# Down projection of the MLP: groups 1 to 3 as seven block products for eight, with the residual rows kept in device memory meanwhile

## The chip, the core and the metric

The kernel runs on one core of a Trainium2 chip. A core has five engines that run their own instruction streams and meet through semaphores: PE (the 128 x 128 matmul array), DVE (element-wise work on two operands), ACT (element-wise work on one operand), POOL and SP (here both only start DMA transfers). The metric is the device time of one execution, in microseconds. Before the change it is 1384.47 us (median of three runs, 1383.11 to 1384.7).

## The reference

One transformer-like block on 512 tokens of width 1024, all in fp32. A gated delta rule with 8 heads and a retention with 4 heads are mixed, and an MLP follows. What matters here is its end:

```
mix = (sigmoid(gate_a) * ya + sigmoid(gate_b) * yb) @ w_out        # w_out 1024 x 1024
x   = x + rmsnorm(mix, n_mix_post)                                 # the residual rows, 512 x 1024
hn  = rmsnorm(x, n_mlp_pre)
ff  = square(relu(hn @ w_up)) @ w_down                             # w_up 1024 x 4096, w_down 4096 x 1024
return x + rmsnorm(ff, n_mlp_post)
```

## The kernel before

**Products.** An fp32 product is emulated by three matmuls (`mm3`, L80): each operand is split into a high part, rounded to the short type fp32r, and a low part, the rest; hi·hi, hi·lo and lo·hi are summed in PSUM. One matmul has a 128 x 128 weight operand and a moving operand of 512 or 256 columns.

**Weights.** All weights stream from device memory in blocks of 512 KB (128 x 1024 fp32, two K tiles of 512 columns). SP starts the load into a tile `raw` (L93, L144), ACT casts the high part `whi` (L110), DVE subtracts to get the low part `wlo` (L111). There are three `whi`/`wlo` pairs in a ring, so a split can be at most three blocks ahead of PE, and two to four `raw` buffers.

**Seven block products.** `seven` (L175) multiplies a 2 x 2 block matrix with seven block products in place of eight (the scheme of Winograd). It needs sums of the quarters of the activations (s1 to s4) and sums of the quarters of the weights (1 to 4). Its products come in a fixed order: 11, s2, 12, s1, s3, 22, s4, two weight blocks each. Quarter (0,0) of the result leaves after "12", (1,1) after "s3", (1,0) after "22" and (0,1) after "s4". Before the change it serves the value and gate projections of the four retention heads, and the up projection of MLP groups 1 to 3.

**Weight sums.** The sums of weight quarters are made in device memory, before they are needed: SP copies a quarter half (512 KB) into a buffer `sums` (L129), and POOL starts a DMA that adds another quarter onto it (L155, `add_blocks`). The copies are paced: `weights` issues one behind each of its loads as long as the list `trickle` is longer than `later_copies[0]`. `later_copies` is 24 at first and 0 from the end of the first retention head on.

**The MLP.** The 4096 hidden columns go in four groups of 1024 (`grp` 0 to 3). In each, the up projection makes squares of relu(hn @ w_up), split into high and low parts as soon as they leave PSUM (`square_relu`, L1101 on: DVE L1105 and L1109, ACT L1108), and the down projection adds squares @ w_down to `facc`. Up of group 0 is plain (`feature_major`), up of groups 1 to 3 runs through `seven`. Down of groups 0 to 2 is plain (`token_major`, L237): eight weight blocks, 24 matmuls of 128x512 for each. Down of group 3 is `row_tiles` (L1007): all weights are split into tiles that stay (`keep`), and each tile of 128 tokens is finished with its norm and its store while the next is multiplied. `row_tiles` also does the product with `w_out` ahead of the MLP; `mix_done` there makes the residual rows `x2` and their normed features `hn`. `x2` stays in the SBUF tile `acc` to the end.

**Order.** A scheduler orders each engine's instructions ahead of time by priorities in program order; `high_priority(n)` moves an instruction forward (weight splits by 200), `keep_in_program_order` pins matmuls, `issue_after` pins a DMA behind another instruction. Each engine then works strictly in that order.

## Time and profile before

| | before |
|---|---|
| median of 3 runs | 1384.47 us |
| profiled execution, its own time | 1384.53 us |
| span of that execution | 1382.8 us |
| PE busy | 1361.0 us, 7102 instructions |
| DVE busy | 923.4 us, 1599 instructions |
| ACT busy | 621.4 us, 1128 instructions |
| moved by DMA | 214.76 MB, mean 155 GB/s |

In the span, up of group 0 runs from about 1028 to 1077 us, down of group 0 to 1121, then up and down of group 1 to 1162 and 1205, of group 2 to 1246 and 1289, up of group 3 to 1329, its down to 1376, and the last norm and stores to the end. The product with `w_out` lies ahead of these, from about 984. Since `grp` counts from 0 and the words of the change from 1, "group 1" of the change is `grp` 0; from here on groups are called by `grp`.

A busy PE in the profile has matmuls in its pipeline, and the durations of single matmuls overlap; what a matmul costs is the pitch in a stage without waits, and not its own duration.

### The profile page before, as it was taken

The page shows a single profiled execution, that of the slowest core. Times are in us where ns is not written, and L with a number is a line of the kernel's source. Part 1 is how long each engine was busy: PE and PEld are TensorE (multiplying, and loading weights), DVE is VectorE, ACT ScalarE, POOL GpSimd, SP SyncE. Part 2 cuts the span into 40 slices and gives each one's busy share as a digit, 9 for nine tenths or more (in the row PEclk, how much of TensorE's full clock was granted, in tenths as well). Part 3 has the DMA queues.
Part 4 walks back from the last instruction along what each step waited for, and adds up shares of the span by engine and source line. Part 5 has one row for each costly group of instructions (what it writes and reads, how often), then busy time and mean ns, then how long its engine had stood idle before and what let it go on. Part 6 is the DMA issues. An engine that isn't in the chain of part 4 may idle for free.

```text
span 1382.8 us, 18650 instructions
## 1 busy us (share of the span) xinstructions
PE 1361.0 (98%) x7102; PEld 1135.8 (82%) x7102; DVE 923.4 (67%) x1599; ACT 621.4 (45%) x1128; POOL 110.5 (8%) x160
## 2 busy tenths in 40 slices
PE   8999999999999999999999999999999999999997
PEld 6888788778887888888888888888888899898986
DVE  5599889963675567567477576675788447374575
ACT  5777564624543323353453343443365444242441
POOL 1112200221011002000000000011011000000000
PEclk9999999999999999999999999999999999999999
DMA  5243625469458447784583873587739645353441
GB/s 160 71 143 116 194 83 170 118 141 240 109 122 161 115 144 167 176 271 155 146 283 90 200 244 104 162 226 156 242 95 226 159 137 153 102 182 113 143 133 61
DMA packets 101660, 214.76 MB, mean 155 GB/s; under 512 B 7135, under 2 KB 20593, under 8 KB 101058
## 3 DMA queue, kind: packets, MB, share of 16 engines
q1 hardware_dynamic: 85616, 170.41, 39.1%
q0 software_dynamic: 15232, 41.90, 16.5%
q8 instruction: 56, 0.92, 0.3%
q10 hardware_dynamic: 722, 1.25, 0.2%
q14 instruction: 34, 0.28, 0.1%
HBM read 207.77 MB, written 64.49 MB: 197 GB/s over the span
## 4 chain that ended last, share of the span: by engine, by line
PE 81%; DVE 9%; DMA 5%; ACT 3%; issue 1%; SPq 0%; DVEq 0%; ACTq 0%
PE mm L83 17%; PE mm L85 17%; PE mm L84 17%; PE mm L827 6%; PE dl L827 5%; PE mm L1127 4%; PE dl L1127 3%; DMA raw<-in_w_in_dram 3%; PE tr L289 2%; DVE wlo L111 2%; DVE c_y L477 1%; ACT whi L110 1%; PE dl L85 1%; PE dl L83 1%; PE dl L84 1%
## 5 line engine op out<-in xcount | busy, mean ns | idle before, releaser
L111 DVE TENSOR_TENSOR wlo<-raw,whi 128x1024 fp32r<-128x1024 f32 x250 | 305.5, 1223 | 293.9 <-ACT whi L110 291.9
L110 ACT CAST whi<-raw 128x1024 fp32r<-128x1024 f32 x250 | 262.8, 1052 | 465.8 <-PE mm L84 190.4
L84 PE MATMUL mm<-actT,whi 128*128 128x512 f32 (+1 forms) x528 | 207.9, 394 | 1.0 <-DVE actT L323 1.0
L85 PE MATMUL mm<-actT,wlo 128*128 128x512 f32 (+1 forms) x528 | 208.8, 396 | 0.0
L83 PE MATMUL mm<-actT,whi 128*128 128x512 f32 (+1 forms) x528 | 207.8, 395 | 0.6 <-ACT actT L322 0.6
L83 PE MATMUL mm<-whi,actT 128*128 128x512 f32 x344 | 136.2, 396 | 0.4 <-DVE r L1105 0.4
L84 PE MATMUL mm<-wlo,actT 128*128 128x512 f32 x344 | 135.8, 395 | 0.0
L85 PE MATMUL mm<-whi,actT 128*128 128x512 f32 x344 | 135.0, 394 | 0.0
L83 PEld LDWEIGHTS mm<-actT,whi 128*128 128x128 f32 x528 | 100.4, 190 | 20.6 <-ACT actT L322 1.1
L84 PEld LDWEIGHTS mm<-actT,whi 128*128 128x128 f32 x528 | 100.4, 190 | 20.2 <-DVE actT L323 1.3
L85 PEld LDWEIGHTS mm<-actT,wlo 128*128 128x128 f32 x528 | 100.6, 191 | 19.0
L83 PE MATMUL mm<-og,whi 128*128 128x512 f32 x256 | 99.8, 390 | 0.1
L84 PE MATMUL mm<-og,whi 128*128 128x512 f32 x256 | 99.7, 389 | 0.0
L85 PE MATMUL mm<-og,wlo 128*128 128x512 f32 x256 | 99.6, 389 | 0.0
L827 PE MATMUL mm<-whi,xsum 128*128 128x512 f32 x256 | 80.8, 389 | 0.0
L83 PEld LDWEIGHTS mm<-whi,actT 128*128 128x128 f32 x344 | 64.6, 188 | 14.6 <-DVE r L1105 0.8
L85 PEld LDWEIGHTS mm<-whi,actT 128*128 128x128 f32 x344 | 64.6, 188 | 13.2
L84 PEld LDWEIGHTS mm<-wlo,actT 128*128 128x128 f32 x344 | 64.6, 188 | 12.8
L477 DVE SCALAR_TENSOR_TENSOR c_y<-c_raw,convw,c_y 128x512 f32<-128x512 f32 x96 | 70.5, 750 | 3.4 <-ACT c_y L475 2.8
L1127 PE MATMUL mm<-hsum,whi 128*128 128x256 f32 x384 | 69.6, 283 | 0.0
L827 PE MATMUL dl<-whi,actT 128*128 128x512 f32 x192 | 61.1, 389 | 0.0
L1127 PEld LDWEIGHTS mm<-hsum,whi 128*128 128x128 f32 x384 | 59.9, 192 | 0.1
(323 smaller groups left out, 2506.1 us busy)
## 6 DMA issues: line engine op xcount, KB each, us to landing
raw<-in_w_in_dram SPq DMA_DIRECT2D x105, 512.0 KB, 4.1
raw<-sums SPq DMA_DIRECT2D x56, 512.0 KB, 3.7
sums<-in_w_in_dram SPq DMA_DIRECT2D x32, 512.0 KB, 5.3
raw<-in_w_down_dram SPq DMA_DIRECT2D x32, 512.0 KB, 4.5
raw<-in_w_up_dram SPq DMA_DIRECT2D x30, 512.0 KB, 3.8
sums<-sums POOLq DMA_DIRECT2D x28, 512.0 KB, 7.4
sums<-in_w_up_dram SPq DMA_DIRECT2D x24, 512.0 KB, 6.8
raw<-in_w_br_a_dram SPq DMA_DIRECT2D x16, 512.0 KB, 4.2
```

The costliest lines, as they stand in the source:

```text
L83: nc.tensor.matmul(ps, lh, rh, start=first, stop=False)
L84: nc.tensor.matmul(ps, lh, rl, start=False, stop=False)
L85: nc.tensor.matmul(ps, ll, rh, start=False, stop=last)
L110: nc.scalar.copy(hi[:, :n], raw[:, :n])
L111: nc.vector.tensor_tensor(lo[:, :n], raw[:, :n], hi[:, :n], ALU.subtract)
L289: nc.tensor.transpose(ps, src, ident)
L477: nc.vector.scalar_tensor_tensor(y, raw[:, j : j + T], tap(j), y, ALU.mult, ALU.add)
L827: m = nc.tensor.matmul(pss[t], lhs[i // 2], rhs[i % 2], start=first and k + i == 0, stop=k + i == 5, skip_group_check=not first,)
L1127: m = nc.tensor.matmul(pss[f // 2][:, ts], lhs[i // 2], rhs[i % 2], start=first and k + i + f % 2 == 0, stop=k + i == 5, skip_group_check= ...
```

## The change

The down projection of groups 0 to 2 runs through `seven` as well: 14 weight blocks of 12 matmuls each (168 matmuls) in place of 8 blocks of 24 (192). What comes with it:

- **Squares.** `Squares` keeps the squares of a group as fp32 in `r4` (four quarters: 11, 12, 21, 22, by token half and hidden half) next to the split quarters 11, 12 and 22, and makes the sums of quarters from them: `first_sums` (L1202 on, of the new kernel: s1, s2, s3, when 21 has left PSUM) and `last_sum` (L1210: s4, when 12 has). Each sum is split too (`split`: ACT cast, DVE L1122). For group 0 all of it is done in two steps of two feature tiles in the end of the plain up projection.
- **Sums of `w_down`.** 24 more copies (SP) and 24 more accumulating DMAs (POOL). `later_copies` is 48, 24 and then, from `w_out` on, 0. So the list that was empty after the attention stages is now worked off behind the eight loads of `w_out`, the twelve loads of up of group 0, and the first ones of its down. The accumulates of `dn0`, `up1`, `dn1`, `up2`, `dn2`, `up3` alternate by group, 18 behind the load of the residual, 8 after up of group 0 and 8 after up of group 1; the load of the last norm's weights comes behind the first 18.
- **Results.** `down_out` adds a quarter of the result to `facc` in one or two steps of 128x512 on DVE (on ACT or DVE for group 0).
- **Residual rows.** `mix_done` also writes each tile of `x2` to `x2_d` in device memory (ACT's queue, 512 KB each). The tile's room (`acc`) then holds sums of hn for the up projections, and before the last down projection POOL's queue loads the four tiles of `x2` back into it.
- **Tiles that stay.** The split weights of `w_out` and of the last down projection go to other tiles (`og`, `s4`, `r4`; `actT`, `s4`, `hn`, `r4`).
- **Sums of hn.** s1 takes the place of quarter 21 of hn itself, so it is written after the last plain up product has read that.

In all, matmuls of 128x512 go from 4602 to 4530, weight splits from 250 to 268, DVE instructions in the program from 1601 to 1689, ACT's from 996 to 1034; SP starts 42 more DMAs and POOL 28 more.

```diff
-    later_copies = [24]
+    later_copies = [48]
...
         if paced and i >= 13 and len(trickle) > later_copies[0]:
-            sums, part, k = trickle.pop(0)
-            with tc.issue_after(load.ins):
-                sums.copy(part, k)
+            copy_block(load)
...
+    def copy_block(load):
+        sums, part, k = trickle.pop(0)
+        with tc.issue_after(load.ins):
+            sums.copy(part, k)
...
     def block_weights(block):
...
-        nc.sync.dma_start(raw.rearrange("p (k c) -> p k c", k=2), block)
+        load = nc.sync.dma_start(raw.rearrange("p (k c) -> p k c", k=2), block)
+        if trickle and not later_copies[0]:
+            copy_block(load)
...
+    def token_product(quarters):
...
+        def product(pss, x, ks, wts, first):
+            wh, wl = wts
+            xh, xl = quarters[x]
+            for t in range(2):
+                tt = slice(t * P, (t + 1) * P)
+                for kk in range(2):
+                    k = 2 * ks + kk
+                    lhs, rhs = (xh[:, k, tt], xl[:, k, tt]), (wh[:, kk, :], wl[:, kk, :])
+                    for i in range(3):
+                        m = nc.tensor.matmul(
...
         def mix_done(t, ps):
             xn = add_normed(t, ps, wpost)
             y = norm_halves([(x2[:, t, hs], lambda half: None) for hs in hss])
+            nc.scalar.dma_start(x2_d[:, t, :], x2[:, t, :])
...
-        keeps = [None] * 3 + og_keeps() + ff_keeps() + facc_keeps()[:1]
+        keeps = [None] * 3 + og_keeps() + s4_keep() + four_keeps(pm, "r4")
+        later_copies[0] = 0
...
+            def first_sums(self, f):
+                fs = slice(f, f + 2)
+                r11, r21, r22 = self.r[:, 0, 0, fs, :], self.r[:, 0, 1, fs, :], self.r[:, 1, 1, fs, :]
+                nc.vector.tensor_tensor(r22, r21, r22, ALU.subtract)
+                nc.vector.tensor_tensor(r21, r11, r21, ALU.subtract)
+                nc.vector.tensor_tensor(r11, r22, r11, ALU.subtract)
+                for r, name in ((r11, "s2"), (r22, "s1"), (r21, "s3")):
+                    split(r, self.fs(name, f))
+
+            def last_sum(self, f):
+                r12 = self.r[:, 1, 0, f : f + 2, :]
+                nc.vector.tensor_tensor(r12, r12, self.r[:, 0, 0, f : f + 2, :], ALU.add)
+                split(r12, self.fs("s4", f))
+
+        def up_out(sq):
+            def out(th, ch, pss, u=(None, None), op=None):
+                for t in range(2):
+                    sq.quarter(ch, th, 2 * t, pss[t], u[t], op)
+                if not sq.last:
+                    for f in (0, 2):
+                        if (th, ch) == (1, 0):
+                            sq.first_sums(f)
+                        elif (th, ch) == (0, 1):
+                            sq.last_sum(f)
...
             if grp < 3:
-                for half in range(2):
-                    pss = token_major(w_down, ff_tile, half * 512, 8, grp * 8)
...
+                src = w_down[grp * D : (grp + 1) * D, :]
+                seven(src, 0, 512, down_sums[grp], token_product(sq.dst), temp, down_out(grp))
             else:
-                wk = og_keeps() + ff_keeps()
+                x2 = cp.tile([P, 4, D], F32, tag="acc", name="x2")
+                for t in range(4):
+                    nc.gpsimd.dma_start(x2[:, t, :], x2_d[:, t, :])
+                wk = four_keeps(act, "actT") + s4_keep()
```

**Order, DVE, where down of group 2 begins.** Weight splits are `wlo`; `r` is a square on its way to `actT`; `dl` and `mm` are PSUM banks; `p1` and `u2` partial sums of `seven`. The first row is the last weight split ahead of the squares that leave after the up product "22". Before:

```order
L111 TENSOR_TENSOR wlo_10025<-raw_10022,whi_10024 128x1024
L1142 TENSOR_TENSOR r_9938<-dl_9876,p1_9540 128x512
L1142 TENSOR_TENSOR r_9943<-dl_9877,p1_9541 128x512
L1105 SCALAR_TENSOR_TENSOR r_9938<-r_9938 128x512
L111 TENSOR_TENSOR wlo_10055<-raw_10052,whi_10054 128x1024
L1109 TENSOR_TENSOR actT_9539<-r_9938,actT_9538 128x2x256
L1105 SCALAR_TENSOR_TENSOR r_9943<-r_9943 128x512
L1142 TENSOR_TENSOR r_10008<-mm_9742,u2_9542 128x512
L111 TENSOR_TENSOR wlo_10085<-raw_10082,whi_10084 128x1024
L1109 TENSOR_TENSOR actT_9539<-r_9943,actT_9538 128x2x256
L1105 SCALAR_TENSOR_TENSOR r_10008<-r_10008 128x512
```

After, at the same place, the middle of the piece: `r4` are the kept squares, `ffq_9625` is s1, `ffq_9627` holds s2 and s3, and the last row begins the squares that leave after the up product "s4" (before: the row with `mm_9742`).

```order
L114 TENSOR_TENSOR wlo_10176<-raw_10173,whi_10175 128x1024
L1204 TENSOR_TENSOR r4_9623<-r4_9623 128x512
L1122 TENSOR_TENSOR ffq_9625<-r4_9623,ffq_9625 128x512
L1205 TENSOR_TENSOR r4_9623<-r4_9623 128x512
L114 TENSOR_TENSOR wlo_10194<-raw_10191,whi_10193 128x1024
L1122 TENSOR_TENSOR ffq_9627<-r4_9623,ffq_9627 128x512 x2
L1204 TENSOR_TENSOR r4_9623<-r4_9623 128x512
L114 TENSOR_TENSOR wlo_10214<-raw_10211,whi_10213 128x1024
L1205 TENSOR_TENSOR r4_9623<-r4_9623 128x512
L1122 TENSOR_TENSOR ffq_9625<-r4_9623,ffq_9625 128x512
L1122 TENSOR_TENSOR ffq_9627<-r4_9623,ffq_9627 128x512 x2
L114 TENSOR_TENSOR wlo_10232<-raw_10229,whi_10231 128x1024
```

Between the squares of "22" and those of "s4" there now stand the sums of the squares, their splits, and more weight splits. In full, from the split of `wlo_10136` (the place of `wlo_10025` before) to the first L1118 on the squares of "s4", DVE has seven weight splits and 21 operations of 128x512.

**Order, DVE, where down of group 0 begins.** Before:

```order
L111 TENSOR_TENSOR wlo_9349<-raw_9346,whi_9348 128x1024
L1109 TENSOR_TENSOR actT_8828<-r_9262,actT_8827 128x512
L1109 TENSOR_TENSOR actT_8828<-r_9267,actT_8827 128x512
L1105 SCALAR_TENSOR_TENSOR r_9272<-mm_9140,r_9272 128x512
L1105 SCALAR_TENSOR_TENSOR r_9277<-mm_9141,r_9277 128x512
L1109 TENSOR_TENSOR actT_8828<-r_9272,actT_8827 128x512
L1109 TENSOR_TENSOR actT_8828<-r_9277,actT_8827 128x512
L111 TENSOR_TENSOR wlo_9379<-raw_9376,whi_9378 128x1024
```

After, the same squares of the second half of the hidden columns: `ffq_8862` holds quarters 12 and 22, `ffq_8863` holds s2 and s3, `ffq_8864` is s4, `ffq_8861` is s1; `hn_8374` is the sum s1 of hn.

```order
L1122 TENSOR_TENSOR ffq_8864<-r4_8859,ffq_8864 128x512
L1115 SCALAR_TENSOR_TENSOR r4_8859<-mm_9165,r4_8859 128x2x256
L114 TENSOR_TENSOR wlo_9448<-raw_9445,whi_9447 128x1024
L1122 TENSOR_TENSOR ffq_8862<-r4_8859,ffq_8862 128x2x256
L1122 TENSOR_TENSOR hn_8374<-full_8858,hn_8373 128x4x256
L1203 TENSOR_TENSOR r4_8859<-r4_8859 128x512
L1204 TENSOR_TENSOR r4_8859<-r4_8859 128x512
L1122 TENSOR_TENSOR ffq_8861<-r4_8859,ffq_8861 128x512
L1205 TENSOR_TENSOR r4_8859<-r4_8859 128x512
L1122 TENSOR_TENSOR ffq_8863<-r4_8859,ffq_8863 128x512
```

The second feature pair's share of s1, s2 and s3 now comes behind all four squares, three weight splits and the first pair's sums.

**Order, SP, at the loads of `w_out`.** Before, the loads follow each other:

```order
L93 DMA raw_8430<-in_w_out_dram 128x1024
L93 DMA raw_8446<-in_w_out_dram 128x1024
L93 DMA raw_8462<-in_w_out_dram 128x1024
L93 DMA raw_8494<-in_w_out_dram 128x1024
L93 DMA raw_8478<-in_w_out_dram 128x1024
```

After, a copy for the weight sums (`sums`) follows each load, and up of group 0 goes on in the same way:

```order
L93 DMA raw_8479<-in_w_out_dram 128x1024
L132 DMA sums_106<-in_w_up_dram 128x2x512
L93 DMA raw_8496<-in_w_out_dram 128x1024
L132 DMA sums_103<-in_w_up_dram 128x2x512
L93 DMA raw_8513<-in_w_out_dram 128x1024
L132 DMA sums_103<-in_w_up_dram 128x2x512
L93 DMA raw_8869<-in_w_up_dram 128x2x512
L132 DMA sums_109<-in_w_down_dram 128x2x512
```

Eight copies stand between and behind the eight loads of `w_out` on SP, and one behind each load of `w_up` that follows.

More of the change, by code (lines that the diff above doesn't have):

```diff
@@ L847, in out @@
                         out1(row, u[t])
-            seven(w_in, c1, c2, sums, product, tmp, out)
+            seven(w_in, c1, c2, sums, token_product(quarters), tmp, out)
         def rotary(pss, dst):
@@ L1145, in hybrid_block_kernel, with temp @@
+        def temp(name):
+            return pm.tile([P, T], F32, tag="u", name=name, bufs=4)
         for grp in range(4):
-            whole = [act.tile([P, 8, T], F32R, tag="actT", name="actT") for _ in range(2)]
-            ff = [[w[:, 4 * half : 4 * half + 4, :] for w in whole] for half in range(2)]
+            sq = Squares(grp)
             if grp:
-                pinned = []
-                seven(
-                    w_up, grp * 1024, grp * 1024 + 512, up_sums[grp - 1], up_product,
-                    lambda name: pm.tile([P, T], F32, tag="u", name=name, bufs=4), squares_up,
-                )
```

192 lines of the change are left out of this document (120 added, 72 removed).

## The prediction

> **What bounds the kernel now.** I read the totals of the page first, then the shares of the chain of waits, then the busy times of the engines stage by stage in the MLP, and last single rows where the change touches them.
>
> ```profile
> span 1382.8 us, 18650 instructions
> ...
> PE 1361.0 (98%) x7102; PEld 1135.8 (82%) x7102; DVE 923.4 (67%) x1599; ACT 621.4 (45%) x1128; POOL 110.5 (8%) x160
> ...
> PE 81%; DVE 9%; DMA 5%; ACT 3%; issue 1%; SPq 0%; DVEq 0%; ACTq 0%
> ```
>
> PE is busy in 98% of the span, and the chain lies on it for 81%. So PE's work is the bound, and a matmul less is worth its pitch, as long as PE still gets its operands in time. The profiled execution took 1384.53 us, 1.7 us more than its span and 0.06 more than the median 1384.47; I sum against 1384.53 and need no correction.
>
> The stages, in columns: stretch, its length, busy time (count) of PE, PEld, DVE, ACT, POOL, granted clock, DMA share, GB/s:
>
> ```profile
> 1028.00:1077.50 49.50, 48.26 (x307) 43.04 (x305) 43.57 (x71) 27.04 (x48) 8.71 (x10) 1.00 0.92 228
> 1077.50:1121.40 43.90, 43.86 (x194) 36.34 (x195) 14.29 (x15) 15.43 (x21) 2.25 (x2) 1.00 0.52 135
> 1121.40:1161.70 40.30, 40.30 (x337) 40.30 (x336) 27.93 (x33) 20.19 (x25) 0.00 (x0) 1.00 0.54 170
> 1161.70:1205.30 43.60, 43.60 (x194) 35.95 (x194) 19.18 (x24) 10.04 (x11) 0.00 (x0) 1.00 0.36 109
> 1245.60:1289.20 43.60, 43.60 (x195) 35.99 (x194) 19.21 (x24) 10.07 (x11) 0.00 (x0) 1.00 0.35 109
> 1329.50:1376.00 46.50, 44.61 (x201) 35.80 (x199) 28.10 (x56) 12.28 (x26) 0.00 (x0) 1.00 0.13 50
> ```
>
> Rows 2, 4 and 5 are the three down projections that change: PE has no gap, and DVE is idle more than half of the time. Row 1, up of group 0, is the tight one: DVE 88% busy, DMA at 0.92.
>
> **Matmuls removed.** A down projection of 192 matmuls takes 43.6 us, so one costs 43.6 / 192 = 0.2271 us. 24 fewer in each of three groups: 72 x 0.2271 = −16.35 us, all on PE and so on the path.
>
> **DVE and ACT work added.** Prices of the kinds that are added, here at the passage from up to down of group 1 (start, duration, engine, line; the last bracket is the wait):
>
> ```profile
> 1156.97 1.23 DVE L111 TENSOR_TENSOR wlo<-raw,whi 128x1024 fp32r<-128x1024 f32 x1
> 1158.11 1.28 DVE L1142 TENSOR_TENSOR r<-dl,p 128x512 f32<-128x512 f32 x2
> 1159.31 0.68 DVE L1105 SCALAR_TENSOR_TENSOR r<-r 128x512 f32<-128x512 f32 x1
> 1159.91 1.22 DVE L111 TENSOR_TENSOR wlo<-raw,whi 128x1024 fp32r<-128x1024 f32 x1
> ...
> 1163.98 0.69 DVE L1109 TENSOR_TENSOR actT<-r,actT 128x512 fp32r<-128x512 f32 x1
> 1164.58 0.69 DVE L1105 SCALAR_TENSOR_TENSOR r<-r 128x512 f32<-128x512 f32 x1
> 1165.18 0.69 DVE L1142 TENSOR_TENSOR r<-mm,u 128x512 f32<-128x512 f32 x1
> ```
>
> ```profile
> 1165.30 0.62 ACT L1108 CAST actT<-r 128x512 fp32r<-128x512 f32 x1 [2.08 <-DVE r L1105]
> 1167.28 0.62 ACT L1108 CAST actT<-r 128x512 fp32r<-128x512 f32 x1 [1.36 <-DVE r L1105]
> ```
>
> Back to back, an operation of 128x512 starts 0.60 us after the one before (1163.98, 1164.58, 1165.18), a weight split 1.135 us. Each group's down gets six more weight splits (6.8 us) and some 24 more operations of 128x512 (sums of squares, their splits, `p1`, `u2`, the second additions to `facc`: 14.4 us), 21 us in all. DVE has 27.93 + 19.18 = 47.1 us of work in the 83.9 us of up and down of group 1; it would have 68 in 78.5, 87%. On average that fits, and I cost it at nothing there; PE's matmuls are its cover. It does not fit where the added work comes in one piece ahead of something that PE needs: the passage from up to down.
>
> **Passage of groups 1 and 2.** Let t = 0 be the end of the up product "22", which the chain shows, with the two stretches of PE behind it:
>
> ```profile
> 1150.16 5.76 PE dl L1127 x48
> 1155.92 5.76 PE mm L1127 x48
> ```
>
> So t = 0 is 1155.92, and PE works on "s4" to 5.76. DVE is 1.05 us late there already (its next split begins at 1156.97). Before, the squares of "s4" are the only thing that PE needs late: the second one's first step on DVE begins at 1165.18 and its cast on ACT is done about 2.7 us later (1167.28 + 0.62), while PE reaches that half of the operands only well into its first weight blocks. After, the order has seven weight splits (7.95 us) and 21 operations (12.6 us) ahead of the cast of the first square of "s4": 1.05 + 20.55 + 0.62 = 22.2, and up to 1 us of waits among DVE, ACT and PE (the `u2` sum waits for PE's product s2, and a split behind it for that product's buffers). PE wants it for down's product "12", which stands behind "11" and "s2", 48 matmuls: 5.76 + 48 x 0.2271 = 16.66. It waits 5.6 to 6.7 us in all, part of it already in "s2", whose sums are on the way. I take 6.3 each, 12.6 for two. The lower bound is 3: ACT and the splits ahead may be overtaken where PE's waits give DVE time; the upper is 9, with one more round of weight splits and casts (1.135 + 0.60 + 0.62) behind it.
>
> **Passage of group 0.** Here there is no product "s4" of up to work on while the sums are made: the plain up ends, all four squares of its second half leave together, and each passes through squares, sums and splits. From the order, 20 operations of 128x512 or alike and 5 weight splits stand up to the second feature pair's split of s2: 12.0 + 5.7 = 17.7 us, begun some 3.5 us before PE ends (the first banks are ready earlier), so 14.2; with cast and waits 15.6. PE wants it half through "s2", behind "11": 36 matmuls, 36 x 0.2271 = 8.2. The wait is 7.4; I take 7.2 (bounds 2 and 10, for the overlap at the start is the part that I know least).
>
> **Copies behind the loads of `w_out`.** Where loads and copies alternate now, the DMA engines are full:
>
> ```profile
> 610.00:620.00 10.00, 10.00 (x46) 8.26 (x44) 9.70 (x13) 5.55 (x8) 0.00 (x0) 1.00 1.01 328
> 980.00:990.00 10.00, 10.00 (x46) 8.11 (x45) 8.90 (x13) 5.44 (x7) 1.05 (x2) 1.00 0.76 216
> 990.00:1000.00 10.00, 9.52 (x42) 7.58 (x41) 4.70 (x5) 3.16 (x3) 1.04 (x2) 1.00 0.89 292
> ```
>
> At 1.01 they move 328 GB/s, so 512 KB (0.524 MB) cost 1.6 us of the queue. At the end of the `w_out` loads, before:
>
> ```profile
> 984.50 3.54 DMA raw<-in_w_out_dram
> ...
> 991.10 5.94 DMA raw<-in_w_out_dram
> 997.07 1.07 ACT keep L110
> 998.16 1.24 DVE keep L111
> 999.43 0.51 PE mm L84
> ```
>
> PE already waits for the last block, which takes 5.94 us. Three copies go ahead of or beside the last loads: up to 3 x 1.6 = 4.8. I take +3, since SP's waits for buffers spread a part of them; bounds 0 (the queue has room in 980 to 990, share 0.76) and 8 (five copies).
>
> **Copies and the `x2` stores in up of group 0.** This stage runs at a share of 0.92 now; twelve copies and the four stores of `x2` bring 16 x 1.6 = 25.6 us more transfers into 50 us, while the accumulates ahead of up of group 1 go on. The `w_up` loads are taken behind buffers that come free at PE's pace, some 5 us ahead of need. I take +2; bounds 0 and 8.
>
> **The last down.** Its 46.5 us hold 43.6 of matmuls, about 0.5 of latency and 2.4 of waits for weights at its start:
>
> ```profile
> 1324.47 4.98 DMA raw<-in_w_down_dram
> ...
> 1331.82 3.75 DMA raw<-in_w_down_dram
> ...
> 1335.32 0.50 PE L84 MATMUL mm<-keep,actT 128*128 128x512 f32 x1 [1.07 <-DVE keep L111]
> ```
>
> The tiles that stay come free earlier now; the reload of `x2` (four transfers, 1.6 us each at the most) runs beside the loads. I take −1.3; bounds −1.8 and +4.
>
> **Costed at nothing.** The accumulates: 24 more on POOL's queue, 7.4 us each at the landing, one behind the other from about 993, make 32 by about 1240, each at least 50 us before its product. The row of the last norm, behind 18 of them, is needed at about 1356. The `x2` stores' issue on ACT: 0.36 us each, in ACT's idle half. The 14 loads of a down in place of 8, 512 KB per 2.7 us of PE, are 40% of the queue. If the accumulates are late, PE waits at "s2" of a down by their lateness.
>
> ```profile
> sums<-sums POOLq DMA_DIRECT2D x28, 512.0 KB, 7.4
> ...
> 1358.82 0.36 ACTq L1193 DMA_DIRECT2D out_dram<-acc  x1
> ```
>
> **Sum.** −16.35 + 12.6 + 7.2 + 3 + 2 − 1.3 = +7.15; 1384.53 + 7.15 = 1391.7, forecast 1392.
>
> **The clock.** What PE's clock does in a long wait is seen at the end of the trace, where it has nothing more to do after a last matmul at 1375.08:
>
> ```profile
> 1372.00:1375.50 3.50, 3.47 (x16) 2.54 (x14) 0.00 (x0) 0.00 (x0) 0.00 (x0) 1.00 0.00 0
> 1375.50:1379.50 4.00, 0.00 (x0) 0.00 (x0) 3.43 (x9) 0.93 (x3) 0.00 (x0) 1.00 0.00 0
> 1379.50:1383.00 3.50, 0.00 (x0) 0.00 (x0) 0.17 (x1) 0.00 (x0) 0.00 (x0) 0.51 0.39 150
> ```
>
> The granted clock is whole for four idle microseconds and half behind them. My waits of 6 to 7 us are in two pieces for groups 1 and 2 (about 2 in "s2", 4 ahead of "12"), on the edge, and in one piece for group 0.
>
> At the start of a run the trace has six matmuls in 2.74 us, 0.43 each, at that half clock:
>
> ```profile
> 1.53 2.74 PE L339 MATMUL dl<-warm 128*128 128x512 bf16 x6 [1.53 <-DVE warm L334]
> ```
>
> If the clock falls, the work behind the wait runs at half speed for as long as the chip needs to give it back, which this trace doesn't bound in the middle of a run; I set one stretch as long as the four idle microseconds, half of it lost: 2 us per wait, 6 for three.
>
> The Trainium skill, "TensorE: Matmul & The Clock Gate", section "Part 1: The HAM clock gate", says that the clock goes to half after an idle window of about 3.4 us and comes back after a busy one of as much; by its figures a wait would cost 1.7 us more, as an estimate, and 5.1 for three. The end of this trace agrees with the first half of it (between 4 and 4.5 us here); no row shows the second in mid-run.
>
> **Rivals.**
>
> *The vector engine keeps up* (faster). If PE's waits are a third of mine, because squares and sums run ahead of my count or DVE gets through splits while PE is fed from the ring, the passages cost 2 to 2.5 each, 7 in all: −16.35 + 7 + 3 + 2 − 1.3 = −5.7, 1379; with the DMA terms at 0 as well 1374. For it speaks DVE's mean load of 87%. Against it speaks that the order is fixed and DVE is unbroken there already before. It decides at waits of (16.35 − 3 − 2 + 1.3) / 3 = 4.2 us per group.
>
> *The clock falls* in the three passages: 1392 + 6 = 1398.
>
> *The transfers starve PE* ahead of the MLP: `w_out` +8 and up of group 0 +8 in place of 3 and 2: 1392 + 11 = 1403. For it speaks the share of 0.92 to 1.01; against, that the loads go ahead of their own copies on SP.
>
> *It comes out even*: gain and waits cancel, 1381.8 to 1387.3. A measurement of this kernel can tell about 0.2%, 2.8 us, from no change.
>
> **How the numbers follow.** Forecast, 1387 to 1396: 0.48. Clock, about 1398: 0.12. Starving, about 1403: 0.12. Even: 0.12. Keeping up, 1374 to 1381: 0.16. Slower by over 0.2% is 0.48 + 0.12 + 0.12 = 0.72, within it 0.12, faster 0.16. The range 1380 to 1404 leaves out the better part of the keeping-up case (0.10) and what goes beyond starving or adds the clock to it (0.08). The likeliest case alone has 1387 to 1396.
>
> **What would show each step.** A down of groups 0 to 2 should take 168 x 0.2271 = 38.2 us of PE work and 44 to 46 of time; PE's idle time at its "s2" and "12" should be ended by DVE's sums and ACT's casts on squares, 6 to 7 us per group, in windows where DVE is over 95% busy. Windows of 10 us should show the granted clock at 1.00 there, or below, for the second rival. In the stage of `w_out` and up of group 0, PE's idle time ahead of weights should grow by 3 and 2 us, with a DMA share of 1. The last down should last about 45 us. Wrong is the forecast if the passages show waits below 4 us each, or if accumulates or the reload of `x2` end waits of PE.

## The result and the profile after

The changed kernel takes 1427.23 us (median of four runs, 1421.54 to 1429.15) against 1384.59 us before: a ratio of 1.0299 with a 95% interval of 1.0266 to 1.0332. It is 3% slower; the forecast was 1392, with a range of 1380 to 1404. The profiled execution took 1421.54 us, span 1419.8.

```profile
span 1419.8 us, 18783 instructions
...
PE 1359.0 (96%) x7030; PEld 1129.4 (80%) x7030; DVE 985.8 (69%) x1687; ACT 649.9 (46%) x1162; POOL 137.2 (10%) x188
...
PE 76%; DVE 12%; DMA 6%; ACT 3%; issue 2%; SPq 0%; DVEq 0%; ACTq 0%
```

PE has 72 instructions less, and is busy only 2 us less: some of its matmuls ran slower. DVE's and DMA's shares of the chain grew.

The stages, cut at the first matmul of each (columns as in the prediction): `w_out`; up and down of group 0; up and down of group 1; down of group 2; the last down.

```profile
979.28:1034.73 55.45, 49.65 (x210) 39.34 (x208) 29.82 (x58) 21.30 (x41) 8.89 (x11) 0.94 1.01 284
1034.73:1096.21 61.48, 52.04 (x306) 46.59 (x304) 44.49 (x77) 27.40 (x51) 8.35 (x9) 0.92 1.04 283
1096.21:1145.10 48.89, 41.09 (x169) 32.49 (x168) 34.11 (x43) 22.86 (x29) 7.83 (x8) 0.93 0.95 236
1145.10:1185.41 40.31, 40.31 (x337) 40.31 (x336) 27.31 (x32) 19.91 (x23) 6.03 (x6) 1.00 1.00 267
1185.41:1234.28 48.87, 41.44 (x170) 32.21 (x169) 41.24 (x55) 21.65 (x26) 6.02 (x6) 0.97 0.87 232
1274.59:1320.45 45.86, 40.90 (x171) 32.13 (x169) 38.86 (x52) 21.36 (x26) 0.00 (x0) 0.96 0.49 160
1360.76:1412.30 51.54, 46.53 (x194) 37.44 (x192) 30.89 (x59) 14.21 (x28) 0.00 (x0) 0.93 0.19 72
```

The first two stages, cut in the same way, before the change:

```profile
982.14:1028.42 46.28, 45.80 (x209) 37.51 (x208) 31.80 (x68) 23.00 (x48) 1.77 (x4) 1.00 0.44 143
1028.42:1077.54 49.12, 47.84 (x306) 42.70 (x304) 43.19 (x71) 27.07 (x47) 8.75 (x10) 1.00 0.92 227
```

`w_out` is 9.2 us longer and its DMA share went from 0.44 to 1.01; up of group 0 is 12.4 longer. The three downs, whose matmuls should take 38.2, take 48.9, 48.9 and 45.9. The granted clock is below 1 in six of the seven stages. From 979 to 1145 the DMA engines are full.

| stage | change predicted | change measured |
|---|---|---|
| `w_out` | +3 | +9.2 |
| up of group 0 | +2 | +12.4 |
| down of group 0 (waits less 5.45 of matmuls) | +1.8 | +5.2 |
| down of group 1 | +0.9 | +5.3 |
| down of group 2 | +0.9 | +2.3 |
| up of group 3, last down | −1.3 | +5.4 |
| ahead of `w_out` | 0 | −2.9 |
| sum (measured: of the spans, within 0.1) | +7.2 | +36.9 |

### The profile page after: what moved, and what is told of

Same layout as the page of the kernel before. It is cut to its first block, busy times and chain, and to the rows that moved or that the text cites. A ratio compares the mean times of both kernels' runs of the same rounds, so it can differ in the third digit from the quotient of the medians.

```text
span 1419.8 us, 18783 instructions
## 1 busy us (share of the span) xinstructions
PE 1359.0 (96%) x7030; PEld 1129.4 (80%) x7030; DVE 985.8 (69%) x1687; ACT 649.9 (46%) x1162; POOL 137.2 (10%) x188
## 4 chain that ended last, share of the span: by engine, by line
PE 76%; DVE 12%; DMA 6%; ACT 3%; issue 2%; SPq 0%; DVEq 0%; ACTq 0%
PE mm L85 14%; PE mm L83 14%; PE mm L84 13%; PE mm L239 10%; PE dl L239 7%; PE mm L1142 4%; PE dl L1142 3%; DVE wlo L114 3%; DMA raw<-in_w_in_dram 3%; PE tr L321 2%; DMA raw<-in_w_up_dram 1%; ACT whi L113 1%; DVE c_y L509 1%; DMA raw<-in_w_out_dram 1%; PE dl L85 1%
## 5 line engine op out<-in xcount | busy, mean ns | idle before, releaser
L114 DVE TENSOR_TENSOR wlo<-raw,whi 128x1024 fp32r<-128x1024 f32 x268 | 327.2, 1222 | 255.5 <-ACT whi L113 252.3
L113 ACT CAST whi<-raw 128x1024 fp32r<-128x1024 f32 x268 | 281.8, 1052 | 459.8 <-PE mm L84 183.5
L239 PE MATMUL mm<-whi,ffq 128*128 128x512 f32 x192 | 63.9, 404 | 12.7 <-ACT ffq L1122 10.1
L164 POOL DMA_DIRECT2D sums<-sums x40 | 33.4, 835 | 376.8 <-DMA sums<-sums 113.1
L83 PE MATMUL mm<-whi,actT 128*128 128x512 f32 x152 | 61.7, 406 | 0.5 <-DVE tb L999 0.5
L84 PE MATMUL mm<-wlo,actT 128*128 128x512 f32 x152 | 61.2, 403 | 0.0
L85 PE MATMUL mm<-whi,actT 128*128 128x512 f32 x152 | 60.7, 401 | 0.0
L239 PEld LDWEIGHTS mm<-whi,ffq 128*128 128x128 f32 x192 | 36.4, 192 | 25.1 <-ACT ffq L1122 12.6
L83 PEld LDWEIGHTS mm<-og,whi 128*128 128x128 f32 x256 | 48.1, 188 | 10.1 <-DVE zz L472 0.4
L85 PEld LDWEIGHTS mm<-og,wlo 128*128 128x128 f32 x256 | 48.1, 188 | 10.1
```

The costliest lines, as they stand in the source:

```text
L83: nc.tensor.matmul(ps, lh, rh, start=first, stop=False)
L84: nc.tensor.matmul(ps, lh, rl, start=False, stop=False)
L85: nc.tensor.matmul(ps, ll, rh, start=False, stop=last)
L113: nc.scalar.copy(hi[:, :n], raw[:, :n])
L114: nc.vector.tensor_tensor(lo[:, :n], raw[:, :n], hi[:, :n], ALU.subtract)
L164: tc.keep_in_program_order(nc.gpsimd.dma_start(dst, src, accum_op=ALU.add))
```

## The experiments

Diffs are against the changed kernel unless something else is said; stage times are those of each run's profile, cut as above. A profile is one execution: with the same code there, down of group 1 takes 46.1 to 50.2 us in the changed kernel and runs 1, 2 and 4 to 6.

**1. The copies earlier.**

```diff
-    later_copies = [48]
+    later_copies = [24]
...
-                later_copies[0] = 24
+                later_copies[0] = 0
...
-        later_copies[0] = 0
         row_tiles(
             w_out,
...
-        if trickle and not later_copies[0]:
-            copy_block(load)
```

> Only the 24 copies that stand behind the loads of w_out, of up of group 0 and in its down are moved: 24 more go behind loads of the gated delta stage, none from w_out on; the number of copies, accumulates and everything else stay. Theory T (the copies fill the DMA queues, and the loads that PE needs come late): 24 x 1.6 us of transfers leave the stretch from 955 to 1110, the loads of w_out and w_up land within 8 us again, and of the some 20 us that PE lost there against before at least 12 come back: 1427 - 15 = about 1412. Rival A (the accumulates on POOL's queue, which start at 987 in place of 1030, fill the queues): less than 5 us come back, about 1424. The waits at the passages to the down projections (some 27 us) stay in either case, but the first one may shrink if late weights have a part in it.

Measured: 1423.93 us (ratio to before 1.0296, 1.0279 to 1.0313). `w_out` took 51.7 and up of group 0 57.7, 3.7 and 3.8 less, but `w_out` began 10 us later: the copies cost elsewhere what they no longer cost here. So 7.5 us of these stages went with the copies, and 14 of the 21.6 stay without them; and moving them earlier is no gain.

**2. The accumulates later.**

```diff
-        add_blocks(residual, 18)
         wpost = broadcast_row(a["norm_mlp_post"][0], "post")
+        with tc.issue_after(rows_in[1].ins):
+            add_blocks(residual, 18)
```

> Only the 18 accumulates behind the residual's loads go back to where before had its accumulates, behind the row of the last norm (about 1030 us). Theory T: the copies stay, the loads of w_out gain a little: 0 to 4 us, about 1425. Rival A (accumulates fill the queues): 10 us or more come back in w_out, about 1415; up of group 0 then pays a part of it again.

Measured: 1422.82 us (1.027, 1.0236 to 1.0303). `w_out` 50.3, so 5.1 less; up of group 0 59.9, 1.5 less. The ratio's interval overlaps that of the changed kernel, so the gain is read from the stage alone: in the five profiles that leave copies and accumulates in place (the changed kernel, runs 3 to 6), `w_out` takes 53.5 to 55.7. The accumulates have a share that I had put at nothing, about half of `w_out`'s loss. Neither they nor the copies are it alone.

**3. The sums of squares wanted later.** In `seven`, for the downs only:

```diff
+        if sums_late:
+            d = bank(psm)
+            summed(d, "22", 4, True)
+            plain(a, "12", 1, c1, False)
+            out(0, 0, a)
+            b = bank(psm)
+            summed(b, "s2", 2, True)
...
+            summed(b, "s3", 3, False)
...
+            out(1, 0, d, p1, ALU.add)
+            e = bank(psx)
+            plain(e, "s4", 1, c2, True)
...
+                    nc.vector.tensor_tensor(u2[t], u2[t], e[t], ALU.subtract)
+            c = bank(psm)
+            summed(c, "s1", 1, True)
+            out(1, 1, c, p1, ALU.subtract)
+            out(0, 1, c, u2, ALU.subtract)
+            return
```

and `first_sums`, `last_sum` follow the squares of all quarters.

> Only the order of the products of the three down projections is changed: 11, 22, 12, s2, s3, s4, s1 in place of 11, s2, 12, s1, s3, 22, s4, with the sums of squares behind all plain squares in program order (and two more DVE operations per group, since s1 and s4 get banks of their own). Theory D (DVE's burst of squares, sums and weight splits ends the waits at the passages): PE wants the sums 11 us later, the waits of 10.4, 10 and 7 us including the half clock behind them fall to 0 to 3 each: 1427 - 20 = about 1407, without a granted clock below 1 there. Rival B (late weights end them, for the queues are full there too, above all for group 0): less than 8 us come back, about 1420 or more.

Measured: 1406.55 us (1.0163, 1.0148 to 1.0178). Down of groups 1 and 2:

```profile
1187.80:1228.05 40.25, 38.70 (x171) 31.31 (x170) 36.54 (x49) 20.51 (x26) 5.03 (x5) 1.00 0.97 253
1268.36:1306.96 38.60, 38.50 (x171) 31.39 (x169) 37.41 (x50) 21.11 (x26) 0.00 (x0) 1.00 0.60 189
```

They fell from 48.9 to 40.3 and from 45.9 to 38.6, at a clock of 1.00; their matmuls are 38.2. DVE's burst of sums was the cause of what went. Down of group 0 came out at 47.7, hardly better. Its longest wait, and what ACT waited for ahead of it:

```profile
PE mm L264 <- DVE u L215: 5.0, 1, 5.0
```

```profile
ACT whi L113 <- DMA raw<-sums: 9.5, 3, 5.5
```

(total, times, longest.) PE waits for DVE's `u2`, which stands behind weight splits whose blocks come late from the DMA: rival B, for this group.

**4. The reload later, first try.** In `row_tiles` of the last down, the four reloads stand behind the loop over its loads, with `issue_after` on the last load, on POOL's queue.

> Only the reload of the four residual tiles is moved behind the last weight load of the last down projection. Theory X (the reload shares the queues with the weight loads, which took 7.8 to 8.8 us beside it in place of 3.7 to 4.2, and PE waits 5.4 us and then runs at half clock): the last stage falls from 51.4 to 45 to 47 us, 1427 - 5 = about 1422. Rival C (PE waits for squares and splits on DVE there, not for loads): no change, 1427.

Measured: 1424.31 us (1.0305, 1.0287 to 1.0324). The reloads were still issued at 1351.8, ahead of six of the eight weight loads: `issue_after` sets the scheduler's order, and POOL's queue waits for nothing on SP's. The run tells nothing of the theory.

**5. The sums of hn held.**

```diff
-                hn_sums()
+                with tc.issue_after(done[1].ins):
+                    hn_sums()
```

where `done` is the last square of the first half of up of group 0.

> Only the sums of hn (13 operations of 128x1024 and smaller on DVE) are held behind the squares of the first half of up of group 0, as before had them; in the changed kernel two of them stand between the norms of the third and the fourth tile of tokens. Theory N (in up of group 0, DVE's order is what PE waits for: the norm of the last tile is done 18 us after the last w_out product in place of 10.5): the waits of up of group 0 fall from about 11 us to 5 or less, 1427 - 6 = about 1421. Theory T (late weight loads end these waits): no change beyond 2 us, 1427.

Measured: 1425.29 us (1.028, 1.0246 to 1.0314). Up of group 0 58.8 in place of 61.5, its down 50.6 in place of 48.9: about 1 us for both together. PE now waits 6.3 us in one piece for the last norm.

**6. The reload on SP's queue**, behind the last weight load, on the same queue.

```diff
-                            nc.gpsimd.dma_start(x2[:, t, :], x2_d[:, t, :])
+                            nc.sync.dma_start(x2[:, t, :], x2_d[:, t, :])
```

> Only the reload of the four residual tiles moves, to SP's queue, where it stands behind the eight weight loads of the last down projection (in the run before, the transfers started at the same time as ever, since POOL's queue does not wait for SP's). Theory X (the reload takes the weight loads' room): these land within 5 us again, the wait of 5.4 us and the half clock behind it go, the last stage falls from 51.2 to 45 to 47 us: 1427 - 5 = about 1422. Rival C (DVE's squares and splits end that wait): no change, 1427.

Measured: 1422.09 us (1.0257, 1.0226 to 1.0287). Up of group 3 and the last down together take 88.7 us to the last matmul, 91.4 in the changed kernel (90.4 to 92.5 in runs 1 to 5, where the reload stays beside the weight loads) and 86.0 before: about half of this loss is the reload's. In what is left, PE's longest wait is 3.2 us, for a square on DVE.

**7. Mended together**: the edits of 2, 3, 5 and 6 ("three parts mended" in the expectations).

> The later sums in the down projections, the held sums of hn, the reload on SP's queue and the accumulates behind 1030 us together; the 24 copies stay behind the loads of w_out and w_up. If the causes are separate, their gains add: 1427 - 20 (passages) - 6 (norms) - 5 (reload) - 4 (accumulates) = about 1392; what stays above 1384.5 - 16.4 = 1368 is then the copies' and the x2 stores' share. If one of them only uncovers another wait, 1400 or more.

Measured: 1394.6 us (1.0062, 1.004 to 1.0083). The gains add. What is left over before lies in `w_out` (52.5), up of group 0 (56.5) and its down (49.2).

**8. The copies in the retention heads**, and 12 accumulates:

```diff
-                later_copies[0] = 24
+                later_copies[0] = 0
...
-                add_blocks(decay, (8, 2, 4)[h - 1])
+                add_blocks(decay, (8, 6, 12)[h - 1])
...
-            add_blocks(residual, 18)
+            add_blocks(residual, 6)
```

on top of run 7, but without the edit of run 2: the six accumulates stand directly behind residual's loads again.

> As the run with three parts mended, but the 24 added copies go behind the block loads of the retention heads 0 to 2, and 12 of the accumulates behind residual's loads go to heads 2 and 3. Theory T: w_out and up of group 0 get their loads as before the change, the heads' DMA share of 0.55 to 0.65 has room: about 1374 to 1380, faster than before the change. If the heads have no room, PE's waits there grow by more than 5 us.

Measured: 1402.89 us (1.012, 1.01 to 1.014). The heads had no room: `w_out` began at 1003.2 in place of 979.3. `w_out` still took 52.0 us, without a copy behind its loads but with accumulates issued beside them, and up of group 0 56.6, although the loads of `w_up` landed in 3.7 to 8.3 us there: neither loss needs the copies. But down of group 0 had none of its waits left, with the sums later and fewer transfers ahead of it (a share of 0.85 in up of group 0, 1.04 in the changed kernel):

```profile
1111.87:1150.05 38.18, 38.18 (x170) 31.46 (x169) 34.51 (x45) 23.27 (x30) 4.53 (x5) 1.00 0.96 255
```

**9. Norms first**: run 7, and `mix_done` under `tc.high_priority(300)`.

> As the run with three parts mended (about 1395), and the norms of the tiles behind w_out get a priority above the weight splits, nothing else. Theory N (in up of group 0, PE waits 6 us for the last tile's norm because DVE's order puts it behind squares and splits): the wait of 6.3 us goes, 1395 - 5 = about 1390. Theory T (DVE is there late because it waits for late weight loads): under 2 us come back.

Measured: 1397.9 us (1.0085, 1.0054 to 1.0116). Nothing came back. PE's longest wait in up of group 0 is still for the last norm, 7.6 us. The priority did not bring all of its steps ahead of the splits: on DVE a weight split at 1050.27, which waited 4.1 us for ACT's cast, still stands in front of the last ones, and ACT waited up to 3.4 us for a load of `w_up`. These loads took up to 20.9 us to land.

**10. Copies later**: run 7, with `later_copies[0] = 0` only ahead of down of group 0, and eight accumulates behind each of down of group 0, up of group 1, down of group 1.

> As the run with three parts mended, but the 24 copies that stood behind the loads of w_out and of up of group 0 go behind the block loads of down of group 0, up of group 1 and down of group 1 (eight each), with eight accumulates behind each; ten accumulates in place of 18 stand ahead of up of group 0. Theory T (the added transfers cost in w_out and up of group 0 what PE waits there): of the waits there (some 6 us in w_out, and those for weights in up of group 0) 5 or more come back: 1395 - 6 = about 1389, if the later stages have room. If the room is missing later too, PE waits at the products of up of group 3 or down of group 2: about 1395 or more.

Measured: 1412.7 us (1.0189, 1.0161 to 1.0216). `w_out` was at 45.7, less than before the change, so its whole loss was the transfers'. Up of group 0, without a copy, still took 56.8. Up of group 1 paid for it:

```profile
1128.21:1183.48 55.27, 46.56 (x336) 44.89 (x337) 30.46 (x36) 18.71 (x22) 7.21 (x7) 0.91 1.04 286
```

55.3 in place of 40.3, at a share of 1.04.

**11. 9 and 10 together.**

> Copies later and norms first together: 1395 - 6 - 5 = about 1384, the same as before the change to within 0.3%; below 1380 only if the waits at up of group 0 had both causes at once.

Measured: 1409.51 us (1.0175, 1.0138 to 1.0212), up of group 1 again some 10 us too long; 3 us less than run 10, which the intervals do not tell apart.

**12. The kernel before, with the copies alone.** Against before:

```diff
         if paced and i >= 13 and len(trickle) > later_copies[0]:
...
+        elif extra:
+            dst, part = extra.pop(0)
+            with tc.issue_after(load.ins):
+                nc.sync.dma_start(dst, part)
```

with 24 blocks of `w_up` in `extra` from `w_out` on, to spare device memory.

> The kernel before, unchanged in what it computes, with 24 copies of 512 KB to device memory that nobody reads, behind the same 24 loads (of w_out, up of group 0 and four more) as in the changed kernel. The price of the copies alone. Theory T: 5 to 12 us, 1384.5 + 8 = about 1392. If the copies find room, 2 us or less: 1386.

Measured: 1398.19 us against 1385.44 (1.0089, 1.0062 to 1.0117): the copies alone cost 12.7 us.

```profile
981.39:1034.60 53.21, 48.13 (x210) 38.55 (x209) 32.17 (x68) 23.11 (x48) 1.78 (x4) 0.97 0.62 216
1034.60:1091.25 56.65, 49.83 (x306) 43.76 (x304) 43.29 (x71) 27.49 (x48) 8.99 (x10) 0.97 1.03 299
1091.25:1134.91 43.66, 43.66 (x193) 36.15 (x193) 14.17 (x15) 15.06 (x20) 1.98 (x2) 1.00 0.53 146
```

`w_out` +6.9, up of group 0 +7.5, down of group 0 unchanged. My terms for both stages, copies and all, were 3 and 2.

**13. One group.** The edits of run 7, and only down of group 2 through `seven`; eight copies and eight accumulates more than before, none of the copies from `w_out` to the end of down of group 0.

```diff
+    in_seven = (2,)
...
-            if grp < 3:
+            if grp in in_seven:
```

> Only down of group 2 runs through seven (sums later, sums of hn held, reload on SP's queue); down of groups 0 and 1 is plain. 8 copies and 8 accumulates more than before in place of 24 and 24: no copy stands behind the loads of w_out and up of group 0, the 8 that are left go behind the block loads of up of group 1, with 8 accumulates behind. Theory T (the added transfers in w_out and up of group 0 are what the change pays most): these stages are as before the change, the gain is 24 x 0.2271 = 5.5 us, less up to 3 for the reload: about 1380 to 1382. If the order on DVE alone keeps PE waiting for the last tile's norm (some 5 us in up of group 0 without any copy there), 1384 to 1387.

Measured: 1391.47 us (1.0044, 1.0029 to 1.0059).

```profile
983.80:1029.64 45.84, 45.75 (x210) 37.49 (x208) 29.71 (x58) 21.22 (x41) 1.77 (x4) 1.00 0.51 173
1029.64:1085.98 56.34, 49.18 (x305) 44.74 (x304) 44.78 (x80) 29.24 (x55) 10.96 (x11) 0.94 0.86 209
```

`w_out` is as before. Up of group 0 is still 7.2 us longer, without a copy and at a DMA share of 0.86 (0.92 before): this part is not the copies'. PE's waits there, and the DVE rows behind the longest of them:

```profile
PE tr L352 <- DVE fw L1131: 6.0, 1, 6.0
PE mm L84 <- DVE fw L1098: 1.2, 1, 1.2
```

```profile
1038.09 1.22 DVE L115 TENSOR_TENSOR wlo<-raw,whi 128x1024 fp32r<-128x1024 f32 x1 [0.17 <-ACT whi L114]
...
1041.79 1.23 DVE L115 TENSOR_TENSOR wlo<-raw,whi 128x1024 fp32r<-128x1024 f32 x1
...
1043.74 1.40 DVE L1103 SCALAR_TENSOR_TENSOR acc<-fw,nr_y,acc 128x512 f32<-128x512 f32 x2
...
1048.76 1.42 DVE L1131 SCALAR_TENSOR_TENSOR fw<-acc,nr_y,wmlp 128x512 f32<-128x512 f32 x2
```

The last tile's norm has four weight splits and some squares between its steps; its last step came at 1048.8, 19 us after the last product of `w_out`; before it was 10.5.

**14. Two groups**: as 13, `in_seven = (1, 2)`, eight copies behind the block loads of up and of down of group 1, accumulates behind each.

> Down of groups 1 and 2 through seven, of group 0 plain; 16 copies and 16 accumulates more than before, eight copies behind the block loads of up of group 1 and eight behind those of down of group 1, accumulates behind each. Theory T: gain 10.9 us, w_out and up of group 0 as in the run with one group, and a part is paid again in up of group 1 and down of group 1, where the transfers now are: 5 to 15 us. About 1380 to 1392; against the run with one group it tells what the second group's transfers cost.

Measured: 1401.89 us (1.0115, 1.0097 to 1.0134). Down of group 1 took 52.5 at a DMA share of 1.05, up of group 1 43.2. The second group costs 10 us more than it saves.

**15. One group, with norms ahead of splits**: run 13, norms with priority, and

```diff
+        if norm_done and next(held) in range(3, 12):
+            with tc.issue_after(norm_done[0].ins):
+                return split_weights(raw, n, nk, keep)
```

in `weights`, where `norm_done` is the last step of the last tile's norm.

> As the run with one group (about 1391), but the norms of the tiles behind w_out have priority and the weight splits of up of group 0 from the fourth on are ordered behind the last tile's norm on DVE and ACT. Theory N (DVE's and ACT's order, in which weight splits that wait for PE's buffers stand ahead of the last norm, ends the waits of 6.3 and 1.5 us and causes the half clock behind them): up of group 0 with its down falls from 99.9 to 93 to 95 us, 1391.5 - 6 = about 1385.5, the same as before the change. If the wait only moves from the norm to the fourth split, 1389 or more.

Measured: 1386.94 us (1.0014, 1.0003 to 1.0026), 4.5 less than run 13.

```profile
1028.59:1081.34 52.75, 48.95 (x305) 44.38 (x304) 43.55 (x72) 27.68 (x50) 9.74 (x11) 0.97 0.91 227
```

Up of group 0 came from 56.3 to 52.8: the order of norms and splits on DVE and ACT is a cause, shown by changing it alone. The other 3.6 us over before stayed; PE's longest wait there is now 2.9 us, for a square on DVE. Down of group 2 saves its 5.0 us (38.6 for 43.6), but up and down of group 1, where the eight copies and eight accumulates now are, take 2.2 and 2.8 more than before, at a DMA share of 0.92 in the up where it was 0.54; what of this the transfers cause was not tested.

**16. All three groups, with norms ahead of splits**: run 7 with the same edit.

> As the run with three parts mended (about 1394.6; all three groups, copies behind w_out and up of group 0), with the same order of norms and splits. Theory N alone: 1394.6 - 6 = about 1389. If late loads end the waits in up of group 0 as soon as the order does not (theory T; a load of w_up took up to 19 us to land there), under 2 us come back, about 1394.

Measured: 1393.57 us (1.0063, 1.0051 to 1.0075), 1 us less than run 7. Beside the added transfers the order gives nothing: up of group 0 took 61.1 us in this profile (of the slowest of the five executions) with loads of `w_up` that took up to 18.3 us to land.

No version beat the kernel before; the best, with one group, is 0.14% behind it.

## Why the prediction was wrong

**Matmuls removed (−16.35): right.** With its waits gone, a down takes 38.2 to 38.6 us (runs 3 and 8), as 168 x 0.2271 gives.

**The passages: the mechanism right, the waits near their size; what follows a wait was left out.** PE's waits at the passages are ended by DVE's and ACT's work on squares. Group 0, PE and then DVE in the changed kernel:

```profile
1105.08 0.39 PE L239 MATMUL mm<-whi,ffq 128*128 128x512 f32 x1
1112.87 0.80 PE L239 MATMUL mm<-whi,ffq 128*128 128x512 f32 x1 [7.41 <-ACT ffq L1122]
1113.47 0.63 PE L239 MATMUL mm<-wlo,ffq 128*128 128x512 f32 x1
...
1117.41 0.40 PE L239 MATMUL mm<-wlo,ffq 128*128 128x512 f32 x1
```

```profile
1107.77 0.68 DVE L1122 TENSOR_TENSOR ffq<-r,ffq 128x512 fp32r<-128x512 f32 x1
1108.37 1.22 DVE L1122 TENSOR_TENSOR hn<-full,hn 128x1024 fp32r<-128x1024 f32 x1
1109.51 0.68 DVE L1203 TENSOR_TENSOR r<-r 128x512 f32<-128x512 f32 x1
...
1111.49 0.68 DVE L1205 TENSOR_TENSOR r<-r 128x512 f32<-128x512 f32 x1
```

The operand came 16.7 us after the end of up (1096.21), where I had 15.6, and PE waited 7.4 where I had 7.2 to 7.4. Group 1:

```profile
1205.05 0.50 PE L239 MATMUL dl<-whi,ffq 128*128 128x512 f32 x1 [3.78 <-ACT ffq L1122]
```

```profile
1183.28 1.22 DVE L114 TENSOR_TENSOR wlo<-raw,whi 128x1024 fp32r<-128x1024 f32 x1
1184.41 1.28 DVE L1117 TENSOR_TENSOR r<-dl,p 128x512 f32<-128x512 f32 x2
```

The end of the up product "22" is 1179.82; the split that I let begin 1.05 us behind it began 3.46 behind. With 2.4 us more, my 22.2 to 23.3 becomes 24.6 to 25.7, and the operand took 25.2 (1205.05). The new work of the passage is not what made DVE late: for group 2 the same split began 1.05 behind and the operand came after 22.8, as I had it. For group 1 weight blocks were late. DVE waited for ACT's casts, and ACT, from 1160 to 1185, for loads:

```profile
ACT whi L113 <- DMA raw<-sums: 5.6, 3, 2.4
ACT whi L113 <- DMA raw<-in_w_up_dram: 3.9, 2, 3.0
```

In run 2, with the same work on DVE there, ACT had no such wait, the split began 1.04 behind, and the stage took 46.1 in place of 48.9. PE's waits add up to 7.8, 7.5 and 5.0 us, where I had 7.2, 6.3 and 6.3; the stages are 10.7, 10.7 and 7.7 over their matmuls (stage less 38.2). About 2.2, 1.7 and 1.5 of that are the clock, below; what is left, about 1 us each, lies at the ends of the waits. For group 0, DVE is not alone: with the sums later there were still 9.5 us, ended by late weight blocks, and they went when copies and accumulates ahead of that stretch were moved (run 8).

**The clock: a rival that belonged into the sum.** I gave it 0.12. Behind the wait of 7.4 us:

```profile
1108.00:1112.80 4.80, 0.00 (x0) 0.00 (x0) 4.77 (x8) 1.89 (x4) 0.00 (x0) 0.74 1.09 279
1112.80:1117.40 4.60, 4.53 (x10) 3.17 (x11) 2.55 (x4) 0.64 (x2) 0.00 (x0) 0.53 1.04 293
1117.40:1120.00 2.60, 2.60 (x13) 2.12 (x12) 1.49 (x2) 1.05 (x1) 0.00 (x0) 1.00 1.02 278
```

Ten matmuls at 0.43 us each in place of 0.23: 2 us per wait. It happened in `w_out`, twice in up of group 0, at all three passages and in the last down: seven stretches at half clock, 37.6 us long, in which PE worked for 30, so some 15 us of the 37. (The granted clocks of the stage rows, length times what is missing to 1, make 18.6 us, PE's waits included.) The estimate of 2 us a wait was right; that there would be seven of them, four outside the passages, was not counted on. The Trainium skill, "TensorE: Matmul & The Clock Gate", section "Part 1: The HAM clock gate", says full clock comes back after a busy window of about 3.4 us. The trace agrees roughly: PE worked 2.9 to 6.2 us at half clock in these stretches.

**Transfers in `w_out` and up of group 0: the step that failed most.** The prediction had 3 + 2, "with bounds 0 and 8" each; measured are 9.2 + 12.4, the second not by transfers alone (next paragraph). The copies alone cost 6.9 + 7.5 (run 12): I counted only the copies directly ahead of the last `w_out` load, and took PE's margin in up of group 0 as 5 us, while a load there took up to 23 us to land. My own figures for that stage did not fit: a share of 0.92 of 49.5 us is 45.5 us of transfers, and the 25.6 that I added make 71 in a stage of 50. The median landing of the 30 `w_up` loads of all groups, before and after (section 6 of the page):

```profile
raw<-in_w_up_dram SPq DMA_DIRECT2D x30, 512.0 KB, 3.8
```

```profile
raw<-in_w_up_dram SPq DMA_DIRECT2D x30, 512.0 KB, 7.7
```

The accumulates were "costed at nothing" because each was in time for its product. They were; but they use the same DMA engines, and where they stand decides about 5 us of `w_out` (run 2). From before to after, section 3 of the page:

```profile
q1 hardware_dynamic: 85616, 170.41, 39.1%
q0 software_dynamic: 15232, 41.90, 16.5%
```

```profile
q1 hardware_dynamic: 93968, 192.44, 42.0%
q0 software_dynamic: 20800, 56.58, 21.9%
```

POOL's queue (q0) took 0.165 x 1382.8 = 228 us of all 16 engines, and 311 after; its 28 additional transfers, 24 of them accumulates, make 83 us, 3 each, against 1.6 for a copy. SP's queue (q1) went from 541 to 596. So more than half of the added DMA time is there, in the term I had left out. Runs 1, 8, 10 and 14 put copies and accumulates at four other places, and each paid at least as much as it saved: at these places, between the heads and down of group 1, there was no such room.

**Up of group 0 had a second cause that I did not see.** Without any added copy there, 7.2 us remained (run 13); the order of the last tile's norm against weight splits is 3.6 of them (run 15). The two causes do not add up: up of group 0 takes 56.7 us with the copies alone (run 12), 56.3 without them (run 13) and 56.5 with both (run 7), so the 12.4 cannot be divided between them, and mending one alone gives little (runs 9, 10 and 16). Nothing in my working looked at what the scheduler does to the norms behind `w_out`. The other 3.6, with the stores of `x2` among what is new there, stays open.

**The last down: wrong sign.** −1.3 predicted, with an upper bound of +4; +5.4 measured. The reload beside the weight loads is about 2.7 (run 6). In the rest PE's wait is ended by a square on DVE (3.2 us in run 6), with half clock behind it; no run changed that alone.

**Costed at nothing and right:** the row of the last norm and the 14 weight loads of a down (40.3 and 38.6 us in run 3). Their share was not the 40% I gave: 1.6 of 2.7 us are 59%, and run 3 shows 0.60 in down of group 2. **The rival "transfers starve PE"** named the place and one of its causes, at two thirds of the price (+11 over the two terms; it was +16.6).

## What to carry to other kernels

A transfer that nobody waits for still has a price: sum the engine time of all added transfers, by kind, over the stretch in which they run, and compare it with the idle share there, before costing any as hidden. A lateness read from the trace of before holds only while the loads ahead of it come as they did: here it held for group 2 and not for group 1. Two causes of one wait do not add up, so removing one may show nothing. If a wait of more than about 2 us enters the sum, the half clock that may follow it belongs in the same term.

## What the runs showed of the hardware that was not expected

Waits much shorter than the four idle microseconds at the end of the trace of before already halve the clock. In run 16, a gap of 3.00 us between two matmul starts, in which PE waited 2.62:

```profile
1344.66 0.39 PE L87 MATMUL mm<-keep,ffq 128*128 128x512 f32 x1
1347.66 0.80 PE L85 MATMUL mm<-keep,ffq 128*128 128x512 f32 x1 [2.62 <-DVE r L1155]
1348.25 0.63 PE L86 MATMUL mm<-keep,ffq 128*128 128x512 f32 x1
1348.68 0.63 PE L87 MATMUL mm<-keep,ffq 128*128 128x512 f32 x1
```

The next matmuls start 0.43 us apart, to 1350.4, where 0.23 returns.

The length of a wait alone does not decide it. In run 13 a wait of 2.29 us (PE back at 1344.37) was followed by half clock, in run 7 one of 2.38 us (back at 1346.38) was not. In the trace of the changed kernel, all changes of the granted clock from `w_out` on lie whole multiples of 3.41 us apart (1004.53, 1011.36, 1042.08, 1045.49, 1055.73, 1062.56, 1110.34, 1117.17 and on), and a stretch at half clock lasts 3.4 or 6.8 us. So where a wait falls in this rhythm seems to count as well; no run tested that by moving a wait.
